# A hybrid decoder layer with 32 routed experts: the load order of the experts is made ahead of the gates, and the affine step of the first LayerNorm moves to GpSimd

## The chip, the cores and the metric

The kernel runs on one core of one Trainium2 chip. The metric is the device time of one execution, in microseconds (us); lower is better. The engines are called by their names here: TensorE (PE in the rows, PEld its weight loads), VectorE (DVE), ScalarE (ACT), GpSimd (POOL) and SyncE (SP), whose queue issues most of the DMA transfers.

## The reference, cut to what matters

One decoder layer on 512 tokens of 1024 channels, all in float32: four token mixers, a LayerNorm, a mixture of experts, a second LayerNorm. Only the end of it bears on this change:

```python
x = layer_norm(alpha * x + m @ w_out, ln1_g, ln1_b)
y = hierarchical_moe(x, ...)              # 32 experts of 1024x512, 1024x512, 512x1024
out = layer_norm(alpha * x + y, ln2_g, ln2_b)

# hierarchical_moe: top-1 of 4 groups, then top-2 of its 8 experts, per token
expert = g_sel * 8 + e_sel                # (512, 2)
gate = pg_top * pe_top / pe_top.sum(-1)
# for each expert e, over the tokens routed to it:
h = silu(xe @ w_gate[e]) * (xe @ w_up[e])
y[token] += gate * (h @ w_down[e])
```

No token is dropped: a loop behind the main part takes what does not fit the places below.

## The kernel before

The mixers and the output product take the first 740 us or so. Then come the experts, in 13 tiles of up to 128 rows (`moe`, L1157). The first two tiles hold the four experts 0 to 3, two experts each with 64 rows, so their weights can be loaded before the routing is known. The other 28 experts are laid on 11 tiles (`TILES`) with strips of 32 to 96 rows; which expert gets which place is decided by its rank when the experts are sorted by how many tokens they have. `K.plan` holds, by place, the rank that the place takes, and its first row and capacity.

For each tile, `expert_block` (L1056) makes the gate product `pg` and the up product `pu` on TensorE, `hh` = Silu(`pg`) * `pu` (Silu on ScalarE, the product on VectorE, L1078), transposes `hh`, makes the down product `py`, and adds it to `acc`, row by row, through a product with the gates (`combine`, L1113; `yh` and `yl` are the two halves of `py` in the format that this product takes). Two callbacks fill the gaps: `early` right behind `hh`, and `late` behind the transposes. In the first tile, `early` makes the gates (`gates`, L878), then the matrices of slots and gates (`slot_gates`, L1000, VectorE only: two comparisons with a slot number, scaled by the gate, and a sum, for each of four token blocks) and the affine step of the first norm, `acc` = ALPHA * (`acc` * g1 + b1) (`affine`, L1847); `late` makes the rest of the routing (`router`, L901). `tc.issue_after(x)` puts what it encloses behind x in the order; the engines' orders come from a scheduler that runs when the kernel is built. Each engine works through its own order and waits where an input or a buffer isn't ready.

The weights come in pieces of 1 MB, six for each expert, on SyncE's queue (`load`, L1725). They turn through 16 buffers, w0 to w15, of which the first ten hold pieces that are loaded during the mixers: piece n goes to buffer n mod 16 as soon as the last product with that buffer's piece is done. Pieces 0 to 11 are those of the first tile (gate 0 to 3, up 4 to 7, down 8 to 11), 12 to 23 of the second, and piece 24 is the first of the routed experts. So piece 24 needs w8, which the down product of the first tile frees halfway, and piece 36 needs w4, which the down product of the second tile frees halfway. From piece 24 on, SyncE reads the number of the expert from `R.order` (`rord`):

```python
es = [num(R.order[0:1, o + i:o + i + 1]) for i in range(ne)]      # L1241
```

In `router`, `rord` comes last of a chain on VectorE, with one product of it on GpSimd (L954): a key for each expert, all pairs of keys compared (28 x 28 on each partition, `rsq`), their sums, which are the ranks, then the base and capacity of each expert, and then the experts by place. The chain stands behind `hh` of the first tile.

Of the kernel before, what the change touches and what calls it, by code (L numbers as in the profile page):

```python
# [7 lines left out]
F32 = mybir.dt.float32  # L8
F32R = mybir.dt.float32r
BF16 = mybir.dt.bfloat16  # L10
I32 = mybir.dt.int32
U32 = mybir.dt.uint32
AF = mybir.ActivationFunctionType
OP = mybir.AluOpType
AX = mybir.AxisListType
PSUM = bass.MemoryType.PSUM

P = 128
# [3 lines left out]
NB = T // P  # L22
ALPHA = 2.0 ** 0.25
# [729 lines left out]
NE = 32  # L753
DE = 512
CAP = 64
NS = 4
ND = NE - NS
# [120 lines left out]
def gates(K, R):  # L878

    V, A = K.nc.vector, K.nc.scalar  # L880
    sb = K.rwk
    s4 = lambda n: sb.tile([P, 4], F32, name=n)
    bc = lambda t, n: t.unsqueeze(2).to_broadcast([P, 4, n])
    gl = R.lg[:, :, 0:4]
    gm, m1, m2 = (R.m[:, i] for i in range(3))
    ge = sb.tile([P, 4, 4], F32, name="rge")
    V.tensor_tensor(ge, gl, bc(gm, 4), op=OP.subtract)
    A.activation(ge, ge, AF.Exp)
    gs = s4("rgs")
    V.tensor_reduce(gs, ge, axis=AX.X, op=OP.add)  # L890
    e2 = s4("re2")
    V.tensor_tensor(e2, m2, m1, op=OP.subtract)
    A.activation(e2, e2, AF.Exp)
    den = s4("rden")
    V.scalar_tensor_tensor(den, e2, 1.0, gs, op0=OP.add, op1=OP.mult)
    R.g = [K.rsb.tile([P, 4], F32, name=f"rgt{j}") for j in range(2)]
    V.reciprocal(R.g[0], den)
    V.tensor_tensor(R.g[1], R.g[0], e2, op=OP.mult)


def router(K, R):  # L901

    nc = K.nc
    V, G, A = nc.vector, nc.gpsimd, nc.scalar
# [2 lines left out]
    OH = [R.oh[:, j] for j in range(2)]  # L907
    pos = R.pos
    cnt = pos[:, 4, :]

    ds_ = slice(NS, NE)
    row = lambda n, w=NE: sb.tile([P, w], F32, name=n)
    key = row("rkey", ND)
    V.scalar_tensor_tensor(key, cnt[:, ds_], float(NE), K.iof[:, ds_], op0=OP.mult, op1=OP.subtract)
    sq = sb.tile([P, ND, ND], F32, name="rsq", tag="rsq", bufs=1)
    V.tensor_tensor(sq, key[:, None, :].to_broadcast([P, ND, ND]), key.unsqueeze(2).to_broadcast([P, ND, ND]),
                    op=OP.is_gt)
    rank = row("rrank", ND)
    V.tensor_reduce(rank, sq, axis=AX.X, op=OP.add)

    at = lambda: V.tensor_tensor(sq, rank[:, None, :].to_broadcast([P, ND, ND]),
                                 K.plan[:, 0].unsqueeze(2).to_broadcast([P, ND, ND]), op=OP.is_equal)
    at()
    V.tensor_tensor(sq, sq, K.plan[:, 1].unsqueeze(2).to_broadcast([P, ND, ND]), op=OP.mult)
    V.tensor_reduce(key, sq.rearrange("p q e -> p e q"), axis=AX.X, op=OP.add)

# [14 lines left out]
    for j in range(2):  # L941
# [7 lines left out]
        V.tensor_tensor(sl, sl, ov, op=OP.add)  # L949
        R.slot.append(sl)  # L950
        lf.append((l_, ov))

    at()
    G.tensor_tensor(sq, sq, K.iof[:, None, ds_].to_broadcast([P, ND, ND]), op=OP.mult)  # L954
    V.tensor_reduce(key, sq, axis=AX.X, op=OP.add)
    R.order = keep.tile([P, ND], I32, name="rord")
    V.tensor_copy(R.order, key)

    nbk, over = row("rnbk"), row("rover")
    V.tensor_tensor(over, cnt, cap, op=OP.subtract)  # L960
# [196 lines left out]
def moe(K, xh, xl, out_acc, R, d0, affine, rest, load, load_rows, load_cols, small, last, ews):  # L1157
# [3 lines left out]
    nc, tc = K.nc, K.tc  # L1161
# [73 lines left out]
    for pr, tl in enumerate(tiles):  # L1235
# [35 lines left out]
        def early(after):  # L1271
            if pr == 0:
                with tc.issue_after(d0[1].end.ins):
                    gates(K, R)
            gts.extend(slot_gates(K, sj, R.g, h * P))
            if end:
                with tc.issue_after(K.send):
                    root()
            if pr == 0:
                with tc.issue_after(K.gend):  # L1280
                    affine()

        def late(after):
            nonlocal xe
# [184 lines left out]
def layer_kernel(tc, a, out):  # L1469
# [12 lines left out]
    with top:  # L1482
# [362 lines left out]
        K.osb = K.rsb  # L1845

        def affine():  # L1847
            for b in range(NB):
                V.scalar_tensor_tensor(acc[:, b, :], acc[:, b, :], ALPHA, g1, op0=OP.mult, op1=OP.mult)
            with tc.issue_after(K.xend):  # L1850
                A.mul(b1, b1, ALPHA)
            for b in range(NB):
                G.tensor_tensor(acc[:, b, :], acc[:, b, :], b1, op=OP.add)
            rst.close()

# [67 lines left out]
```

## Time and profile before

| | us |
|---|---|
| median of 3 runs | 1234.81 (1234.26 to 1236.95) |
| the profiled execution | 1239.61 |
| its span | 1237.8 |
| busy in the span: TensorE | 1150.0 (93%) |
| VectorE | 644.8 (52%) |
| ScalarE | 352.8 (29%) |
| GpSimd | 139.4 (11%) |

All rows are of the profiled execution, with times from the start of its span. A timeline row gives the start, the length, the engine, the line and the operation with its output and inputs; x4 behind it means four instructions merged, and then the length goes from the first start to the last end. A length includes what an instruction waits after it has begun. Starts and lengths are the profiler's; where one ends after the next has begun, the two overlap in the engine's pipeline.

### The profile page before, as it was taken

The numbers are of one execution on the slowest core, as the hardware profiler recorded it, in microseconds if no ns is written. First come the engines' busy times: TensorE is split into PE (matmuls) and PEld (weight loads), VectorE is DVE, ScalarE is ACT, GpSimd is POOL, SyncE is SP. The second block draws the span as 40 slices with busy tenths as digits, with TensorE's granted clock in tenths as the row PEclk, the third lists the DMA queues.
The fourth block names the chain that finished last, engine by engine and source line by source line (L and its number), as shares of the span: only waits on it lengthen the run. The fifth ranks groups of instructions, "written<-read, shape, count | busy, mean of one in ns | idle before, by whom it ended". The sixth has DMA issues, their size and how long they took to land.

```text
span 1237.8 us, 18955 instructions
## 1 busy us (share of the span) xinstructions
PE 1150.0 (93%) x6991; PEld 777.0 (63%) x6991; DVE 644.8 (52%) x1769; ACT 352.8 (29%) x752; POOL 139.4 (11%) x192
## 2 busy tenths in 40 slices
PE   7999999999999999999999988998999789987993
PEld 6768788888876776888888983532544234532542
DVE  6488878522239884334435489751444224432247
ACT  5433434333334444333334452100111011110012
POOL 4021322100000000212211044000000000000003
PEclk9999999999999999999999998999999999999996
DMA  7311212456652111656553238899999999999991
GB/s 185 89 41 33 44 29 70 132 181 192 188 177 64 52 36 40 216 162 192 179 172 122 94 116 326 348 421 420 421 422 420 421 420 421 421 421 421 420 340 70
DMA packets 108699, 276.65 MB, mean 224 GB/s; under 512 B 19393, under 2 KB 74780, under 8 KB 86076
## 3 DMA queue, kind: packets, MB, share of 16 engines
q1 hardware_dynamic: 90604, 252.79, 54.8%
q10 hardware_dynamic: 16768, 19.82, 5.0%
q0 software_dynamic: 1232, 2.81, 0.7%
q8 instruction: 56, 0.92, 0.3%
q14 instruction: 39, 0.32, 0.1%
HBM read 263.71 MB, written 11.67 MB: 222 GB/s over the span
## 4 chain that ended last, share of the span: by engine, by line
PE 68%; DMA 17%; DVE 9%; issue 2%; ACT 1%; POOL 1%; SPq 1%; ACTq 0%; DVEq 0%; POOLq 0%
PE mm L1382 9%; PE mm L1380 9%; PE mm L1381 9%; DMA w<-in_e_gate 6%; PE pu L1071 5%; DMA w<-in_e_down 5%; PE py L1101 4%; PE pg L1071 4%; DMA w<-in_e_up 3%; PE pm L1034 2%; PE pm L1036 2%; PE pm L1116 1%; PE pm L1117 1%; PE po L1705 1%; PE po L1706 1%
## 5 line engine op out<-in xcount | busy, mean ns | idle before, releaser
L1154 DVE TENSOR_TENSOR wlo<-wraw,whi 128x512 fp32r<-128x512 f32 (+2 forms) x180 | 123.1, 686 | 194.8 <-ACT whi L1151 193.3
L1380 PE MATMUL mm<-xh,whi 128*128 128x512 f32 x496 | 200.1, 404 | 2.5 <-ACT pc L1535 1.4
L1382 PE MATMUL mm<-xh,wlo 128*128 128x512 f32 x496 | 201.3, 406 | 0.0
L1381 PE MATMUL mm<-xl,whi 128*128 128x512 f32 x496 | 199.1, 401 | 0.0
L1151 ACT CAST whi<-wraw 128x512 fp32r<-128x512 f32 (+2 forms) x180 | 109.9, 612 | 205.9 <-PE mm L1381 142.1
L1124 DVE TENSOR_TENSOR acc<-acc,pm 128x512 f32<-128x512 f32 (+1 forms) x106 | 64.3, 655 | 111.3 <-PE pm L1117 111.3
L1101 PE MATMUL py<-w,hT 128*32 128x512 f32 (+2 forms) x608 | 114.8, 578 | 7.5 <-DMA w<-in_e_down 7.2
L1071 PE MATMUL pu<-w,xe 128*32 128x512 f32 (+1 forms) x576 | 104.6, 596 | 12.9 <-DMA w<-in_e_up 12.9
L1071 PE MATMUL pg<-w,xe 128*32 128x512 f32 (+1 forms) x576 | 101.4, 598 | 10.0 <-DMA w<-in_e_gate 10.0
L1380 PEld LDWEIGHTS mm<-xh,whi 128*128 128x128 f32 x496 | 94.1, 190 | 25.9 <-ACT pc L1535 2.7
L1382 PEld LDWEIGHTS mm<-xh,wlo 128*128 128x128 f32 x496 | 94.0, 190 | 22.3 <-issue 1.6
L1381 PEld LDWEIGHTS mm<-xl,whi 128*128 128x128 f32 x496 | 94.2, 190 | 21.7 <-issue 1.7
L1101 PEld LDWEIGHTS py<-w,hT 128*32 128x32 f32 (+1 forms) x608 | 35.2, 123 | 78.1 <-issue 56.4
L1071 PEld LDWEIGHTS pu<-w,xe 128*32 128x32 f32 (+1 forms) x576 | 29.2, 121 | 80.5 <-issue 54.9
L1071 PEld LDWEIGHTS pg<-w,xe 128*32 128x32 f32 (+1 forms) x576 | 30.6, 122 | 76.0 <-issue 55.0
L1034 PE MATMUL pm<-D,xh 128*128 128x256 f32 (+1 forms) x224 | 53.9, 283 | 1.2 <-DVE D L995 1.2
L1036 PE MATMUL pm<-D,xl 128*128 128x256 f32 (+1 forms) x224 | 53.8, 283 | 0.0
L1122 POOL TENSOR_TENSOR acc<-acc,yo 128x256 f32<-128x256 f32 x6 | 4.3, 732 | 438.2 <-ACT yo L1121 438.2
L1078 DVE TENSOR_TENSOR hh<-hh,pu 128x512 f32<-128x512 f32 x13 | 8.9, 686 | 79.6 <-PE pu L1071 79.6
L1109 ACT ACTIVATE yh<-py,dg 128x512 fp32r<-128x512 f32 x24 | 16.5, 686 | 116.3 <-PE py L1101 99.6
L1711 POOL TENSOR_TENSOR mT<-mT,th 128x512 f32<-128x512 f32 x24 | 35.7, 1486 | 123.6 <-DVE th L1710 122.6
L1401 PE MATMUL mm<-wlo,xh 128*128 128x256 f32 (+1 forms) x160 | 46.7, 292 | 0.0
(640 smaller groups left out, 2040.3 us busy)
## 6 DMA issues: line engine op xcount, KB each, us to landing
w<-in_e_gate SPq DMA_DIRECT2D x60, 1024.0 KB, 19.8
w<-in_e_down SPq DMA_DIRECT2D x58, 1024.0 KB, 19.8
w<-in_e_up SPq DMA_DIRECT2D x58, 1024.0 KB, 19.8
wraw<-in_w_in SPq DMA_DIRECT2D x128, 256.0 KB, 2.9
w<-in_e_up SPq DMA_DIRECT2D x12, 512.0 KB, 15.9
w<-in_e_down SPq DMA_DIRECT2D x12, 512.0 KB, 8.4
wraw<-in_w_branch SPq DMA_DIRECT2D x16, 256.0 KB, 2.6
w<-in_e_gate SPq DMA_DIRECT2D x8, 512.0 KB, 5.3
```

Source lines behind the costliest of these rows:

```text
L1034: TE.matmul(ps[:, i, :], self.xh[:, kt, b * P:b * P + P], D[:, b, :], start=i == 0 and b == 0, stop=False, skip_group_check=True)
L1036: TE.matmul(ps[:, i, :], self.xl[:, kt, b * P:b * P + P], D[:, b, :], start=False, stop=i == per - 1 and b == NB - 1, skip_group_check=True)
L1071: end = TE.matmul(ps[c, :], xe[:, kt, c], w(e, kind, kt, 0, T), start=kt == 0, stop=kt == 7, skip_group_check=True)
L1101: TE.matmul(at(c0, c1)[c, :], hT[:, f, c], w(e, 2, f, c0, c1), start=f == 0 and c0 % T == 0, stop=f == 3 and c1 % T == 0, skip_group_check ...
L1124: V.tensor_tensor(o, o, ps, op=OP.add)
L1151: nc.scalar.copy(hi, src)
L1154: nc.vector.tensor_tensor(lo, src, hi.bitcast(F32), op=OP.subtract)
L1380: TE.matmul(ps[i], hi[:, k, cs], self.xh[:, kk, :], start=kk == 0, stop=False)
L1381: TE.matmul(ps[i], hi[:, k, cs], self.xl[:, kk, :], start=False, stop=False)
L1382: end = TE.matmul(ps[i], lo[:, k, cs], self.xh[:, kk, :], start=False, stop=kk == 7)
L1401: TE.matmul(ps[:, :n], self.xh[:, kk, s], lo[:, k, :], start=False, stop=False)
L1711: G.tensor_tensor(mT[:, j, :], mT[:, j, :], th, op=OP.add)
```

## The change

Three things are moved. The ranks and the load order become a function of their own, `load_order`, which runs ahead of `gates` on VectorE, right behind the last `xe` (the gathered inputs of the experts); it works on the 28 x 28 pairs in two halves, and its one product on GpSimd becomes VectorE's. `router` keeps only the bases and capacities, from the ranks that are there. The affine step leaves VectorE: ScalarE scales both g1 and b1 by ALPHA, right behind its last `xe`, and GpSimd multiplies `acc` by one and adds the other. It no longer stands behind the slot gates.

```diff
--- before.py
+++ after.py
@@ -898,6 +898,35 @@
     V.tensor_tensor(R.g[1], R.g[0], e2, op=OP.mult)
 
 
+def at_place(K, R, sq, places=slice(0, ND)):
+
+    K.nc.vector.tensor_tensor(sq, R.rank[:, None, :].to_broadcast(sq.shape),
+                              K.plan[:, 0, places].unsqueeze(2).to_broadcast(sq.shape), op=OP.is_equal)
+
+
+def load_order(K, R):
+
+    V = K.nc.vector
+    sb, keep = K.rwk, K.rsb
+    ds_ = slice(NS, NE)
+    key = sb.tile([P, ND], F32, name="rkey")
+
+    V.scalar_tensor_tensor(key, R.pos[:, 4, ds_], float(NE), K.iof[:, ds_], op0=OP.mult, op1=OP.subtract)
+    nh = ND // 2
+    sq = sb.tile([P, nh, ND], F32, name="rsqh")
+    R.rank = keep.tile([P, ND], F32, name="rrank")
+    for h in (slice(0, nh), slice(nh, ND)):
+        V.tensor_tensor(sq, key[:, None, :].to_broadcast([P, nh, ND]), key[:, h].unsqueeze(2).to_broadcast([P, nh, ND]),
+                        op=OP.is_gt)
+        V.tensor_reduce(R.rank[:, h], sq, axis=AX.X, op=OP.add)
+    for h in (slice(0, nh), slice(nh, ND)):
+        at_place(K, R, sq, h)
+        V.tensor_tensor(sq, sq, K.iof[:, None, ds_].to_broadcast([P, nh, ND]), op=OP.mult)
+        V.tensor_reduce(key[:, h], sq, axis=AX.X, op=OP.add)
+    R.order = keep.tile([P, ND], I32, name="rord")
+    K.oend = V.tensor_copy(R.order, key).ins
+
+
 def router(K, R):
 
     nc = K.nc
@@ -907,20 +936,11 @@
     OH = [R.oh[:, j] for j in range(2)]
     pos = R.pos
     cnt = pos[:, 4, :]
-
     ds_ = slice(NS, NE)
     row = lambda n, w=NE: sb.tile([P, w], F32, name=n)
     key = row("rkey", ND)
-    V.scalar_tensor_tensor(key, cnt[:, ds_], float(NE), K.iof[:, ds_], op0=OP.mult, op1=OP.subtract)
     sq = sb.tile([P, ND, ND], F32, name="rsq", tag="rsq", bufs=1)
-    V.tensor_tensor(sq, key[:, None, :].to_broadcast([P, ND, ND]), key.unsqueeze(2).to_broadcast([P, ND, ND]),
-                    op=OP.is_gt)
-    rank = row("rrank", ND)
-    V.tensor_reduce(rank, sq, axis=AX.X, op=OP.add)
-
-    at = lambda: V.tensor_tensor(sq, rank[:, None, :].to_broadcast([P, ND, ND]),
-                                 K.plan[:, 0].unsqueeze(2).to_broadcast([P, ND, ND]), op=OP.is_equal)
-    at()
+    at_place(K, R, sq)
     V.tensor_tensor(sq, sq, K.plan[:, 1].unsqueeze(2).to_broadcast([P, ND, ND]), op=OP.mult)
     V.tensor_reduce(key, sq.rearrange("p q e -> p e q"), axis=AX.X, op=OP.add)
 
@@ -949,12 +969,6 @@
         V.tensor_tensor(sl, sl, ov, op=OP.add)
         R.slot.append(sl)
         lf.append((l_, ov))
-
-    at()
-    G.tensor_tensor(sq, sq, K.iof[:, None, ds_].to_broadcast([P, ND, ND]), op=OP.mult)
-    V.tensor_reduce(key, sq, axis=AX.X, op=OP.add)
-    R.order = keep.tile([P, ND], I32, name="rord")
-    V.tensor_copy(R.order, key)
 
     nbk, over = row("rnbk"), row("rover")
     V.tensor_tensor(over, cnt, cap, op=OP.subtract)
@@ -1271,14 +1285,15 @@
         def early(after):
             if pr == 0:
                 with tc.issue_after(d0[1].end.ins):
+                    load_order(K, R)
+                with tc.issue_after(K.oend):
                     gates(K, R)
             gts.extend(slot_gates(K, sj, R.g, h * P))
             if end:
                 with tc.issue_after(K.send):
                     root()
             if pr == 0:
-                with tc.issue_after(K.gend):
-                    affine()
+                affine()
 
         def late(after):
             nonlocal xe
@@ -1845,11 +1860,11 @@
         K.osb = K.rsb
 
         def affine():
-            for b in range(NB):
-                V.scalar_tensor_tensor(acc[:, b, :], acc[:, b, :], ALPHA, g1, op0=OP.mult, op1=OP.mult)
             with tc.issue_after(K.xend):
+                A.mul(g1, g1, ALPHA)
                 A.mul(b1, b1, ALPHA)
             for b in range(NB):
+                G.tensor_tensor(acc[:, b, :], acc[:, b, :], g1, op=OP.mult)
                 G.tensor_tensor(acc[:, b, :], acc[:, b, :], b1, op=OP.add)
             rst.close()
 
```

VectorE's order behind the gathered inputs `xe`, before. `rge`, `re`, `rgs`, `rden` and `rgt` are the steps of the gates, `g` and `G` those of the slot gates.

```order
L1047 TENSOR_SCALAR xe<-pm,ln1c 128x256 x4
L887 TENSOR_TENSOR rge<-lg,rm_6901 128x16
L892 TENSOR_TENSOR re_7851<-rm_6901 128x4
L890 TENSOR_REDUCE rgs<-rge 128x4
L895 SCALAR_TENSOR_TENSOR rden<-re_7851,rgs 128x4
L897 RECIPROCAL rgt_7856<-rden 128x4
L898 TENSOR_TENSOR rgt_7857<-rgt_7856,re_7851 128x4
L1009 TENSOR_SCALAR g_7860<-iof,rsl_6900,rgt_7856 128x128
```

The same place now, up to the load order:

```order
L914 SCALAR_TENSOR_TENSOR rkey<-rpos,iof 128x28
L919 TENSOR_TENSOR rsqh<-rkey 128x392
L921 TENSOR_REDUCE rrank<-rsqh 128x14
L919 TENSOR_TENSOR rsqh<-rkey 128x392
L921 TENSOR_REDUCE rrank<-rsqh 128x14
L903 TENSOR_TENSOR rsqh<-rrank,plan 128x392
L924 TENSOR_TENSOR rsqh<-rsqh,iof 128x392
L925 TENSOR_REDUCE rkey<-rsqh 128x14
L903 TENSOR_TENSOR rsqh<-rrank,plan 128x392
L924 TENSOR_TENSOR rsqh<-rsqh,iof 128x392
L925 TENSOR_REDUCE rkey<-rsqh 128x14
L927 CAST rord<-rkey 128x28
```

Eleven instructions and the cast to `rord` stand between `xe` and the first step of the gates (`rge`, which follows next).

VectorE's order around `hh` of the first tile, before:

```order
L1011 TENSOR_TENSOR G<-G,g_7870 128x128
L1009 TENSOR_SCALAR g_7875<-iof,rsl_6900,rgt_7856 128x128
L1011 TENSOR_TENSOR G<-G,g_7875 128x128
L1849 SCALAR_TENSOR_TENSOR acc<-acc,g_7788 128x1024 x4
L1009 TENSOR_SCALAR g_8087<-iof,rsl_6900,rgt_7856 128x128
L1078 TENSOR_TENSOR hh<-hh,pu 128x512
L914 SCALAR_TENSOR_TENSOR rkey<-rpos,iof 128x28
L928 TENSOR_SCALAR rbase<-iof 128x4
L929 MEMSET rcap 128x4
L916 TENSOR_TENSOR rsq<-rkey 128x784
```

And now:

```order
L1025 TENSOR_TENSOR G<-G,g_7886 128x128
L1023 TENSOR_SCALAR g_7891<-iof,rsl_6900,rgt_7872 128x128
L1025 TENSOR_TENSOR G<-G,g_7891 128x128
L1023 TENSOR_SCALAR g_8095<-iof,rsl_6900,rgt_7872 128x128
L1092 TENSOR_TENSOR hh<-hh,pu 128x512
L903 TENSOR_TENSOR rsq<-rrank,plan 128x784
L948 TENSOR_SCALAR rbase<-iof 128x4
L949 MEMSET rcap 128x4
L944 TENSOR_TENSOR rsq<-rsq,plan 128x784
```

The four affine steps ahead of `hh` are gone, and so are the key `rkey` and the first comparisons behind it.

GpSimd's order at the affine step, before (`xl` belongs to the norm, the product with `iof` to the load order, the last row to the last tile):

```order
L1440 DMA g_7788<-in_ln_g 128x1024
L1440 DMA b_7789<-in_ln_b 128x1024
L1801 TENSOR_TENSOR xl<-acc,xh 128x8x64 x2
L1853 TENSOR_TENSOR acc<-acc,b_7789 128x1024 x4
L954 TENSOR_TENSOR rsq<-rsq,iof 128x784
L1122 TENSOR_TENSOR acc<-acc,yo 128x256 x6
```

And now:

```order
L1455 DMA g_7788<-in_ln_g 128x1024
L1455 DMA b_7789<-in_ln_b 128x1024
L1816 TENSOR_TENSOR xl<-acc,xh 128x8x64 x2
L1867 TENSOR_TENSOR acc<-acc,g_7788 128x1024 x2
L1868 TENSOR_TENSOR acc<-acc,b_7789 128x1024 x2
L1867 TENSOR_TENSOR acc<-acc,g_7788 128x1024 x2
L1868 TENSOR_TENSOR acc<-acc,b_7789 128x1024 x2
L1136 TENSOR_TENSOR acc<-acc,yo 128x256 x6
```

Eight affine instructions stand there instead of four, with nothing of VectorE's ahead of them. SyncE's order stays as it was. On TensorE one group moves: the products of the first tile's first `combine` stand behind three products of the second tile's `pu`, and not behind eleven.

## Rows read from the trace of the kernel before

**Rows 1.** The page of the kernel before: what the DMA engines moved in each of the 40 slices of the span (31 us each), and the pieces of gate weights that SyncE issues at L1729.

```profile
GB/s 185 89 41 33 44 29 70 132 181 192 188 177 64 52 36 40 216 162 192 179 172 122 94 116 326 348 421 420 421 422 420 421 420 421 421 421 421 420 340 70
...
w<-in_e_gate SPq DMA_DIRECT2D x60, 1024.0 KB, 19.8
```

**Rows 2.** Three stretches of the span: length, then busy time and instructions of each engine, the granted share of TensorE's full clock, the mean share of the 16 DMA engines, and what they moved.

```profile
768.50:777.50 9.00, 9.00 (x46) 2.93 (x44) 9.00 (x26) 0.00 (x0) 1.85 (x1) 1.00 0.02 7
777.50:805.00 27.50, 26.36 (x150) 15.74 (x148) 19.71 (x65) 4.71 (x8) 0.00 (x0) 1.00 0.99 399
805.00:1195.00 390.00, 351.79 (x2074) 153.67 (x2068) 142.10 (x326) 39.84 (x65) 0.00 (x0) 1.00 1.01 419
```

**Rows 3.** Who waited for whom on SyncE's DMA queue, over the whole span: total us, times, longest us.

```profile
SPq L1164 <- DVE rlf L945: 18.0, 1, 18.0
...
SPq L1729 <- PE py L1101: 17.4, 11, 12.0
```

**Rows 4.** SyncE's timeline: start and length in us, the issues merged. The last row is from a narrower window.

```profile
753.93 4.24 SPq L1729 DMA_DIRECT2D w<-in_e_down  x4
776.66 6.58 SPq L1729 DMA_DIRECT2D w<-in_e_gate  x8
...
805.03 0.91 SPq L1729 DMA_DIRECT2D w<-in_e_up  x2
```

**Rows 5.** VectorE's timeline from the end of the gathered inputs on: start, length, line, operation, and in brackets idle time of the engine just before.

```profile
742.08 1.96 DVE L1047 TENSOR_SCALAR xe<-pm,ln1c 128x256 f32<-128x256 f32 x4 [0.90 <-PE pm L1036]
743.95 0.17 DVE L887 TENSOR_TENSOR rge<-lg,rm 128x16 f32<-128x16 f32 x1
746.20 0.17 DVE L890 TENSOR_REDUCE rgs<-rge 128x4 f32<-128x16 f32 x1 [2.01 <-ACT rge L888]
746.97 0.34 DVE L1009 TENSOR_SCALAR g<-iof,rsl,rgt 128x128 f32<-128x128 f32 x1
...
750.33 8.95 DVE L1849 SCALAR_TENSOR_TENSOR acc<-acc,g 128x1024 f32<-128x1024 f32 x4
759.20 2.36 DVE L1009 TENSOR_SCALAR g<-iof,rsl,rgt 128x128 f32<-128x128 f32 x1
761.48 0.67 DVE L1078 TENSOR_TENSOR hh<-hh,pu 128x512 f32<-128x512 f32 x1
762.08 1.75 DVE L914 SCALAR_TENSOR_TENSOR rkey<-rpos,iof 128x28 f32<-128x28 f32 x1
...
766.85 0.96 DVE L921 TENSOR_TENSOR rsq<-rrank,plan 128x784 f32<-128x784 f32 x1
...
772.00 1.92 DVE L1010 TENSOR_SCALAR G<-iof,rsl,rgt 128x128 f32<-128x128 f32 x1
...
775.70 0.16 DVE L957 CAST rord<-rkey 128x28 int32<-128x28 f32 x1
...
776.08 0.40 DVE L962 TENSOR_TENSOR ro<-rover,thr 128x256 f32<-128x256 f32 x1
```

**Rows 6.** TensorE's timeline: up product of the first tile, transposes of `hh`, down products of the first and of the second tile.

```profile
750.30 7.04 PE L1071 MATMUL pu<-w,xe 128*64 128x512 f32 x32
...
762.21 1.13 PE L1083 MATMUL pm<-ident,hh 128*128 128x128 f32 x4 [4.02 <-DVE hh L1078]
...
765.89 8.33 PE L1101 MATMUL py<-w,hT 128*64 128x512 f32 x32
...
801.36 7.09 PE L1101 MATMUL py<-w,hT 128*64 128x512 f32 x32
```

**Rows 7.** ScalarE's timeline.

```profile
742.65 1.99 ACT L1045 ACTIVATE xe<-pm,ln1c 128x256 f32<-128x256 f32 x4 [5.33 <-DVE xe L1047]
...
746.17 1.04 ACT L1851 ACTIVATE b<-b 128x1024 f32<-128x1024 f32 x1
...
780.81 0.68 ACT L1109 ACTIVATE yh<-py,dg 128x512 fp32r<-128x512 f32 x1
```

**Rows 8.** GpSimd's timeline; the two rows of L1853 are from narrower windows, each of two instructions of the four.

```profile
727.92 3.11 POOL L1801 TENSOR_TENSOR xl<-acc,xh 128x512 fp32r<-128x512 f32 x2 [5.92 <-ACT xh L1800]
...
736.32 3.16 POOL L1801 TENSOR_TENSOR xl<-acc,xh 128x512 fp32r<-128x512 f32 x2 [0.91 <-DVE roh L858]
...
754.86 6.62 POOL L1853 TENSOR_TENSOR acc<-acc,b 128x1024 f32<-128x1024 f32 x2
...
758.15 5.64 POOL L1853 TENSOR_TENSOR acc<-acc,b 128x1024 f32<-128x1024 f32 x2
...
771.99 1.85 POOL L954 TENSOR_TENSOR rsq<-rsq,iof 128x784 f32<-128x784 f32 x1 [8.20 <-DVE rsq L921]
```

**Rows 9.** VectorE's timeline: single instructions beside GpSimd's. The last row is from a narrower window.

```profile
730.16 0.19 DVE L845 TENSOR_REDUCE rm<-rel 128x1 f32<-128x32 f32 x1
...
736.52 1.42 DVE L857 TENSOR_TENSOR rohs<-rel,rel 128x32 bf16<-128x32 f32 x1
737.87 1.66 DVE L859 TENSOR_TENSOR roh<-rel,rel 128x32 f32<-128x32 f32 x1
...
755.91 3.37 DVE L1849 SCALAR_TENSOR_TENSOR acc<-acc,g 128x1024 f32<-128x1024 f32 x1
```

**Rows 10.** Two stretches of one microsecond, columns as in rows 2.

```profile
762.00:763.00 1.00, 0.79 (x4) 0.79 (x5) 1.00 (x2) 0.00 (x0) 1.00 (x1) 0.50 0.96 401
...
768.00:769.00 1.00, 1.00 (x6) 0.26 (x4) 1.00 (x3) 0.00 (x0) 0.00 (x0) 0.76 0.46 188
```

## The prediction

> **What bounds the kernel now.** Read first the page's slices: TensorE looks like the bound, but the rate of the DMA engines tells more [rows 1]. From slice 26 to slice 37 (counting from 0) it stands at 420 to 422 GB/s; the two slices ahead of that have only 326 and 348. The table of stretches makes both exact [rows 2]: from 805 to 1195 us the sixteen DMA engines are full (share 1.01, 419 GB/s), and from 768.5 to 777.5 us they move next to nothing (7 GB/s). The full stretch is the stream of expert weights, in pieces of 1024 KB (1.049 MB), so 2.5 us each at 419 GB/s. A stream that never pauses again hands every delay at its head to the end of the kernel, and every gain too. So the question is when the stream starts, and whether it stays full.
>
> Next, SyncE's queue, which issues the stream. Its longest wait there is 18.0 us for `rord`, the load order (the view names a VectorE neighbour, L945), and then 12.0 us for the down product `py` of the second tile [rows 3]. In order of time [rows 4]: the last four pieces of fixed experts go out from 753.93 to 758.17, the first routed piece (piece 24, counting from 0) at 776.66, and piece 36 at 805.03. In between, 399 GB/s over 27.5 us [rows 2] is what a full stream moves in 26.2 us, so the routed stream counts as full from 778.8, 2.1 us behind its first issue. Twelve pieces (24 to 35) last to 808.8; piece 36 was issued 3.8 us ahead of that, 1.7 us earlier than it had to be. The head of the stream thus has two conditions: piece 24 needs the order and slot w8, which the first tile's `py` frees; piece 36 needs w4, which the second tile's `py` frees.
>
> Third, VectorE, on whose queue both hang [rows 5]. `xe` is done about 744; gates and slot gates follow (the last from 746.97 to 750.33); four affine instructions 750.33 to 759.28; one more slot gate 2.36; then `hh` at 761.48, on which TensorE waits: its up product ended at 757.34, and the transposes of `hh` start at 762.21, `py` at 765.89 [rows 6]. `rord` is written at 775.70, last of a chain begun at 762.08.
>
> **The change, part by part.** *The order goes ahead of the gates.* The twelve instructions cost 5.8 us by themselves: a 784-element comparison takes 0.96 and a 256-element one 0.40 [rows 5], so 0.55 for the 392 of a half (estimated between the two); ten of these make 5.5, the key and the cast 0.16 to 0.17 each like their narrow neighbours. With nothing in the way `rord` would stand at 749.8, and even with the waits below at about 757.5, when SyncE is still issuing fixed pieces (to 758.17). So the wait of 18.0 us is gone. The next thing that is late is w8. In the router behind `hh`, the key, one square, two reductions, one comparison and the cast fall away; nothing on TensorE waits there soon enough to count, so I book nothing.
>
> *The affine moves to GpSimd.* VectorE loses 8.95 us ahead of `hh`. GpSimd gets eight instructions of 128x1024 instead of four, and no longer waits for VectorE: ScalarE scales g1 right behind its last `xe` (744.64), one such product takes 1.04 [rows 7], so GpSimd starts at 745.75, while VectorE is in the middle of the order. That start decides, because the two engines do not run side by side here. GpSimd's third affine ends at 761.48 and its fourth at 763.79 [rows 8]; VectorE's fourth affine lasts from 755.91 to 759.28, 3.37 long, and ends 1.1 behind 758.15, where GpSimd's second ends and its third begins [rows 8, 9]. The slot gate at 759.20 takes 2.36 instead of 0.34 and ends with GpSimd's third; the key at 762.08 takes 1.75 for 28 elements and ends with its fourth. A 0.34 us gate at 772.00 takes 1.92 beside a GpSimd product of 1.85 [rows 5, 8]. And they take turns: of two adjacent comparisons of 32 elements, the one at 736.52 ends with the first of two GpSimd instructions and the one at 737.87 with the second [rows 8, 9]. Not all are held: the reduction at 730.16 takes 0.19 inside a GpSimd instruction, and `hh`, one of whose inputs lies in PSUM, takes 0.67 at 761.48 [rows 5, 8, 9].
>
> GpSimd's own time for 128x1024 follows from the turns: 761.48 less 759.28 is 2.20, 763.79 less 761.56 is 2.23. I take 2.2, so eight are 17.6 us.
>
> Now the sum for `hh`. VectorE's own work from 743.95 to `hh` is 10.6: order 5.8, six gate instructions 1.0, slot gates 3.4 (746.97 to 750.33), one more 0.3, rounding. Of that, 1.8 runs before GpSimd starts; 2.2 (three half reductions, the cast, a narrow reduction, the reciprocal) runs beside it; 2.7 (four half comparisons and products at 0.55, three narrow ones at 0.17) gets one turn each between GpSimd's eight; 3.9 follows. So `hh` starts at 745.75 + 17.6 + 2.7 + 3.9 = 770.0 instead of 761.48: **8.5 us later**, though VectorE has less to do. ScalarE's two exponentials, the table loads around them and the Silu fit into the waits.
>
> TensorE's steps behind `hh` move with it. Its clock fell in the idle time before the transposes to 0.50, its 1.2 GHz level, and came back to 2.4 GHz within 768 to 769, after six microseconds of work [rows 10]; I take the same after the longer pause. Full-speed `py` is 7.09 [rows 6], so half of the first one was done at 765.89 + 8.33 - 3.5 = 770.7, now 779.2; 2.1 behind that the stream is full at 781.3 (before: 778.8), and twelve pieces last to 811.3. Piece 36: 805.03 + 8.5 = 813.5, and 0.7 more, as the first combine now stands after three products of the second tile's up product and not eleven, while `yh` still follows that tile's Silu (780.81 before) [rows 7]; with 2.1 that is 816.3, against 808.8. The stream pauses a second time, and what follows is **7.5 us late**. Behind that the slots are freed in time: piece 40 needed only the next gate product, nine microseconds later too, with four pieces of 2.5 us ahead of it.
>
> The profiled execution took 1239.61 us, 4.8 more than the median of the runs, 1234.81; the difference is added to the median: 1234.8 + 7.5 = **1242.3**.
>
> Ends of this sum: without the 0.7, and 1.5 for the 2.1, it is +6.2. If GpSimd's products cost what 1.85 for 784 elements [rows 8] scales to, 2.4, four of eight give 0.8 more; if the clock stays low through all of the first `py`, some 2 us more. So +5 to +10: 1240 to 1245.
>
> The page "SBUF — State Buffer" of the Trainium skill, section "SBUF: two separate sides", states that VectorE and GpSimd share one pair of ports under an exclusive lock held for a whole instruction, by VectorE for two SBUF inputs or a two-port mode. The rows agree in what is held (the slot gate's 2.36) and what not (`hh`, 0.67). It does not say who is next: taken without turns, it leads to the third rival.
>
> **The rivals.** *One, faster: VectorE goes first.* If its instructions passed GpSimd's whenever they were ready, or GpSimd's started late, the order, gates and slot gates would end by 754.6 (756.6 with the 2.0 wait for the exponential [rows 5]) and `hh` would wait only for the up product: 757.4, 4.1 earlier than now. TensorE would hardly idle, its clock would stay up, and about 3.0 come back (1.2 in `py`, half of the 3.7 between the transposes and `py`). Piece 36 is then ready at 805.0 - 4.1 - 3.0 + 0.7 + 2.1 = 800.7; the fixed pieces' stream ends at 768.5 and twelve more at 798.5. Gain 8.1: 1226.7. For it: the hole of 9 us is real and the order is early enough. Against it: every turn in [rows 8, 9]. It decides at the break-even point, `hh` 1.0 later than now, 762.5. Chance 0.15.
>
> *Two, no change: several VectorE instructions per turn.* With four, about half of GpSimd's work is passed before `hh`, which comes near 762; piece 36 starts about where it does now: 1235. For it: the turns seen are few; against it, the two adjacent comparisons did not pass together. Chance 0.08.
>
> *Three, slower still: no turns.* GpSimd's eight hold VectorE from its first held instruction, 746.4, to 763.35, and 8.2 to 8.6 of its work follow: `hh` at 772, 10.5 late, the stream 9.5: 1244.3. The two adjacent comparisons speak against it [rows 9]. Chance 0.12.
>
> **How the numbers follow.** The forecast has 0.65. A measurement tells about 0.2% (2.5 us) from no change; forecast and third rival are slower by more, 0.77; faster 0.15; same 0.08. The range 1232 to 1246 holds the forecast with its ends and rivals two and three, and leaves out the faster case.
>
> **What would show it.** In the profile after: SyncE waits for the first `py`, not for `rord`; GpSimd's affine starts near 745.8 and ends near 766; VectorE's half comparisons and gates last 2 us and more, one per GpSimd instruction; `hh` near 770, piece 24 near 779, piece 36 near 814, with a short pause of the DMA engines ahead of it; then 419 GB/s to the end. I am wrong if `hh` comes before 763, or if the second pause is missing.

## The result, and the profile after

The changed kernel is slower: median 1245.16 us (four runs, 1242.50 to 1246.02) against 1234.85, a ratio of 1.0073 with a 95% interval of 1.0055 to 1.0091. Twelve later runs of the same kernel, again beside the kernel before, gave 1.0045 (1.0025 to 1.0065). So the loss is between 3 and 11 us; the forecast was 7.5. One of the twelve runs of the kernel called e4_vector_only below took 2557.12 us, where the others lie between 1229.45 and 1239.03, and stands in no ratio; why it took so long isn't shown.

The profiled execution took 1244.92 us, its span 1243.2. It ended its `xe` 0.5 us earlier than the profile of before (743.54 against 744.04, from VectorE's rows), so times of the two traces are compared from there. First the stretches of the DMA engines, which answer to [rows 2] (same columns):

```profile
768.50:778.00 9.50, 8.46 (x34) 3.75 (x36) 9.33 (x33) 0.58 (x1) 0.00 (x0) 0.73 0.01 3
778.00:808.80 30.80, 29.50 (x164) 16.61 (x162) 17.24 (x55) 4.70 (x8) 0.00 (x0) 1.00 1.00 408
808.80:812.70 3.90, 3.90 (x22) 1.33 (x20) 3.90 (x15) 0.00 (x0) 0.00 (x0) 1.00 0.19 36
812.70:1195.00 382.30, 344.88 (x2044) 151.49 (x2040) 137.77 (x317) 37.13 (x61) 0.00 (x0) 1.00 1.01 418
```

The pause at the head is still there, and a second one has opened from 808.8 to 812.7, where before the stream was full. Next SyncE's timeline (the last row from a narrower window), which answers to [rows 4], and then who waited for whom on its queue from 740 to 815 us (total, times, longest), which answers to [rows 3]:

```profile
753.43 4.24 SPq L1744 DMA_DIRECT2D w<-in_e_down  x4
777.03 9.77 SPq L1744 DMA_DIRECT2D w<-in_e_gate  x8
...
811.49 0.91 SPq L1744 DMA_DIRECT2D w<-in_e_up  x2
```

```profile
SPq L1744 <- PE py L1115: 36.3, 4, 18.1
...
SPq L1178 <- DVE rge L887: 0.7, 1, 0.7
```

Nothing of any length waits for the order any more (0.7 us, named by a VectorE neighbour). The wait of 18.0 us is gone, and one of 18.1 us for the first tile's `py` stands in its place. Counted from the end of `xe`, piece 24 goes 33.5 us later (before 32.6), and piece 36, the row at 811.49, 68.0 us (before 61.0). Now the timelines of VectorE, which answers to [rows 5], and of GpSimd, which answers to [rows 8]:

```profile
746.06 2.01 DVE L903 TENSOR_TENSOR rsqh<-rrank,plan 128x392 f32<-128x392 f32 x1
748.11 2.60 DVE L924 TENSOR_TENSOR rsqh<-rsqh,iof 128x392 f32<-128x392 f32 x1
750.75 0.56 DVE L925 TENSOR_REDUCE rkey<-rsqh 128x14 f32<-128x392 f32 x1
751.34 2.02 DVE L903 TENSOR_TENSOR rsqh<-rrank,plan 128x392 f32<-128x392 f32 x1
753.39 2.60 DVE L924 TENSOR_TENSOR rsqh<-rsqh,iof 128x392 f32<-128x392 f32 x1
...
756.63 1.61 DVE L927 CAST rord<-rkey 128x28 int32<-128x28 f32 x1
758.16 0.16 DVE L887 TENSOR_TENSOR rge<-lg,rm 128x16 f32<-128x16 f32 x1
758.24 2.30 DVE L892 TENSOR_TENSOR re<-rm 128x4 f32<-128x4 f32 x1
...
760.82 2.03 DVE L895 SCALAR_TENSOR_TENSOR rden<-re,rgs 128x4 f32<-128x4 f32 x1 [0.19 <-ACT re L893]
...
763.09 2.06 DVE L898 TENSOR_TENSOR rgt<-rgt,re 128x4 f32<-128x4 f32 x1
...
768.80 0.68 DVE L1092 TENSOR_TENSOR hh<-hh,pu 128x512 f32<-128x512 f32 x1
```

```profile
745.21 5.07 POOL L1867 TENSOR_TENSOR acc<-acc,g 128x1024 f32<-128x1024 f32 x2 [6.25 <-issue]
...
760.49 4.64 POOL L1868 TENSOR_TENSOR acc<-acc,b 128x1024 f32<-128x1024 f32 x2
```

On VectorE read the lengths, which no longer go by the size: a half comparison takes 2.01, a half reduction 0.56, and the 4-element subtraction at 758.24 takes 2.30. Eight are long (all rows but the reduction, `rge` and `hh`), as many as GpSimd has, and GpSimd's eight last from 745.21 to 765.13, without a gap. None of the eight reads or writes a tile that GpSimd's do, so what holds them is no input. One more passed: `rge`, with two inputs in the SBUF, took 0.16 right behind the held cast. After 765.13 nothing is held, and `hh` comes 3.7 us later. TensorE's timeline, which answers to [rows 6], and two stretches that answer to [rows 10]:

```profile
762.75 1.97 PE L1085 MATMUL pg<-w,xe 128*64 128x512 f32 x2 [5.91 <-ACT hh L1091]
769.54 1.12 PE L1097 MATMUL pm<-ident,hh 128*128 128x128 f32 x4 [4.83 <-DVE hh L1092]
...
773.21 7.22 PE L1115 MATMUL py<-w,hT 128*64 128x512 f32 x32
...
807.81 7.09 PE L1115 MATMUL py<-w,hT 128*64 128x512 f32 x32
```

```profile
760.00:773.00 13.00, 5.42 (x14) 2.40 (x16) 12.43 (x26) 2.67 (x4) 5.12 (x3) 0.50 0.63 263
773.00:774.00 1.00, 1.00 (x6) 0.38 (x4) 1.00 (x2) 0.00 (x0) 0.00 (x0) 0.71 0.00 0
```

TensorE stood idle for 5.91 us ahead of the first row and for 4.83 more ahead of the transposes of `hh`. Its granted clock was 0.50, its 1.2 GHz level, from 760 to 773, and came back with the first products of `py`, which took 7.22. The second `py` starts at 807.81, 64.3 us after `xe` (before 57.3).

### The profile page after: what moved, and what is told of

Its sections match the earlier page's. It is cut to its first block, busy times and chain, and to the rows that moved or that the text cites. A ratio compares the mean times of both kernels' runs of the same rounds, so it can differ in the third digit from the quotient of the medians.

```text
span 1243.2 us, 18962 instructions
## 1 busy us (share of the span) xinstructions
PE 1149.6 (92%) x6991; PEld 776.8 (62%) x6991; DVE 648.3 (52%) x1771; ACT 353.4 (28%) x753; POOL 144.6 (12%) x195
## 4 chain that ended last, share of the span: by engine, by line
PE 67%; DMA 20%; DVE 8%; issue 2%; POOL 1%; ACT 1%; SPq 0%; ACTq 0%; DVEq 0%; POOLq 0%
PE mm L1397 9%; PE mm L1395 9%; PE mm L1396 9%; DMA w<-in_e_gate 6%; DMA w<-in_e_down 6%; DMA w<-in_e_up 5%; PE py L1115 4%; PE pu L1085 4%; PE pg L1085 4%; PE pm L1048 2%; PE pm L1050 2%; PE mm L1416 1%; PE po L1720 1%; PE po L1721 1%; PE po L1719 1%
## 5 line engine op out<-in xcount | busy, mean ns | idle before, releaser
L1138 DVE TENSOR_TENSOR acc<-acc,pm 128x512 f32<-128x512 f32 (+1 forms) x106 | 64.3, 656 | 112.2 <-PE pm L1131 112.2
L1115 PE MATMUL py<-w,hT 128*32 128x512 f32 (+2 forms) x608 | 111.4, 574 | 5.6 <-DMA w<-in_e_down 5.3
L1396 PEld LDWEIGHTS mm<-xl,whi 128*128 128x128 f32 x496 | 94.4, 190 | 21.6 <-issue 1.5
## 6 DMA issues: line engine op xcount, KB each, us to landing
w<-in_e_gate SPq DMA_DIRECT2D x60, 1024.0 KB, 19.8
w<-in_e_down SPq DMA_DIRECT2D x58, 1024.0 KB, 19.8
w<-in_e_up SPq DMA_DIRECT2D x58, 1024.0 KB, 19.9
```

Of the source, the lines that this page charges most:

```text
L1115: TE.matmul(at(c0, c1)[c, :], hT[:, f, c], w(e, 2, f, c0, c1), start=f == 0 and c0 % T == 0, stop=f == 3 and c1 % T == 0, skip_group_check ...
L1138: V.tensor_tensor(o, o, ps, op=OP.add)
L1396: TE.matmul(ps[i], hi[:, k, cs], self.xl[:, kk, :], start=False, stop=False)
```

## The experiments

All counts below start at the end of the first `xe`, since the stretch ahead of it varies from run to run. "Without loads" is what is missing from a full DMA share in the 100 one-microsecond stretches from there, and "last load" is the first issue behind the last expert's weights. In the three runs e4 and e8, two of the 32 products of the second `py` go some 10 us ahead of the rest; the column has the start of the other 30. Ratios are against runs of the kernel before on the same chip; 0.001 is 1.24 us.

| run | `hh` | piece 24 | second `py` | last load | us without loads | ratio, 95% interval |
|---|---|---|---|---|---|---|
| before | 17.4 | 32.6 | 57.3 | 452.0 | 11.0 | |
| e0_before_again | 17.4 | 32.6 | 58.9 | 451.5 | 10.5 | 0.9992, 0.9976 to 1.0009 |
| after | 25.3 | 33.5 | 64.3 | 457.8 | 15.0 | 1.0073, 1.0055 to 1.0091 |
| after_again | 25.3 | 34.0 | 64.7 | 458.3 | 15.6 | 1.0045, 1.0025 to 1.0065 |
| e1_order_only | 19.7 | 27.6 | 60.4 | 453.9 | 11.4 | 1.0016, 1.0001 to 1.0032 |
| e2_affine_only | 23.2 | 37.8 | 62.5 | 456.7 | 15.4 | 1.0043, 1.0028 to 1.0058 |
| e3_no_affine | 13.5 | 19.9 | 50.6 | 443.9 | 2.3 | 0.9949, 0.9930 to 0.9968 |
| e6_four_on_gpsimd | 18.1 | 26.0 | 55.9 | 449.1 | 6.2 | 0.9982, 0.9962 to 1.0002 |
| e7_memset | 13.7 | 20.1 | 50.9 | 444.3 | 2.6 | (one run) |
| e4_vector_only | 13.4 | 19.8 | 55.0 | 447.6 | 5.5 | 0.9979, 0.9958 to 1.0000 |
| e4_again | 13.4 | 19.8 | 54.8 | 447.6 | 5.7 | 0.9977, 0.9959 to 0.9995 |
| e8_two_ahead | 13.4 | 19.8 | 51.5 | 443.9 | 2.0 | 0.9931, 0.9910 to 0.9951 |

The theory: VectorE and GpSimd take turns, one held instruction of VectorE's for each of GpSimd's, and `hh` and all behind it pay for that. The main rival: the order step itself costs, by the VectorE work that it puts ahead of `hh`.

### The two kernels once more

> The kernel before, unchanged, for a second profile. Its first profiled execution took 1239.6 us where the runs of it have their median at 1234.85, so the profiles of before and after lie 5.3 us apart and the medians 10.3. If that first profile was the odd one, this one takes about 1235 us, with `hh` still near 761.5, piece 24 near 776.7 and piece 36 near 805.0 counted from its own start, and the missing 5 us show in one other stretch. If a profile of this kernel always costs it some 5 us, it comes out near 1239.6 again. The ratio to itself should be 1.000, within 0.002.

> The kernel after, unchanged, in more runs and for a second profile. Its four runs gave +10.3 us by the medians (ratio 1.0073, from 1.0055 to 1.0091), while its trace, counted from the end of `xe` to the last load, is only 5.9 us longer than that of the kernel before (457.8 against 452.0), with 15.0 us without loads against 11.0. If the trace holds all of the loss, the ratio comes out near 1.005, the low edge of the first interval. If some 3 to 4 us of the loss lie elsewhere, it stays near 1.007, and a second profile shows a longer stretch ahead of `xe` or behind the last load than those of the kernels before.

The second profiled execution of before took 1240.5 us, but the median of that kernel's runs is 1236.0: neither was a median run. Their stages agree where it counts (`hh` at 17.4, 11.0 and 10.5 us without loads). Not all repeats: in the second, TensorE waited 1.66 us for `yl` (0.35 in the first), the second `py` came 1.6 us later, and piece 36 went 62.6 us after `xe` (61.0), which cost nothing visible, as the first profile left piece 36 1.7 us to spare. Most of what differs between runs lies ahead of `xe`: its end stood between 738.7 and 746.3 us in the twelve profiles of this study, in code that is the same up to there. The second profile of after repeats the first to 0.6 us in every column. So the trace shows a loss of 5.8 to 6.8 us (457.8 and 458.3 against 452.0 and 451.5), and the runs' 9.0 and 5.6 (ratio less 1, times 1236) lie on both sides of it. The new ratio is the 1.005 that was expected if the trace holds all of the loss. Why the first four runs gave 3 us more isn't shown; the two intervals overlap.

### The order alone

```diff
 # the affine step as in the kernel before; the order ahead of the gates as after
+for b in range(NB):
+    V.scalar_tensor_tensor(acc[:, b, :], acc[:, b, :], ALPHA, g1, ...)
 with tc.issue_after(K.xend):
-    A.mul(g1, g1, ALPHA)
     A.mul(b1, b1, ALPHA)
 for b in range(NB):
-    G.tensor_tensor(acc[:, b, :], acc[:, b, :], g1, op=OP.mult)
     G.tensor_tensor(acc[:, b, :], acc[:, b, :], b1, op=OP.add)
...
-    affine()
+    with tc.issue_after(K.gend):
+        affine()
```

> The order step ahead of the gates as in the kernel after; the affine step as before (four VectorE instructions behind the slot gates, four additions on GpSimd). Theory (the time is lost because GpSimd's eight products and sums hold VectorE): without them the half order step costs VectorE about 10.6 us ahead of `hh`, of which some 9 come back since the affine work no longer stands ahead of it; `hh` near 763, piece 24 near 777.5, time 0 to +2 us against before. Rival (the order step itself is what costs, since it puts some 10 us of VectorE ahead of the gates and of all that TensorE waits for): `hh` near 769 as in the kernel after, time +6 us or more.

Measured +2.0 us (0.1 to 4.0), `hh` at 19.7 where the theory had 19 and the rival 25. The rival falls as the main cause; a small cost is left. Piece 24 came 5 us earlier than before, which the expectation had wrong (it had it later), and nothing was gained by it. The timelines of VectorE and TensorE in this run, and one stretch with the columns of [rows 2]:

```profile
759.02 2.54 DVE L903 TENSOR_TENSOR rsq<-rrank,plan 128x784 f32<-128x784 f32 x1
761.48 2.31 DVE L948 TENSOR_SCALAR rbase<-iof 128x4 f32<-128x4 f32 x1
...
779.43 1.34 PE L1131 MATMUL pm<-yl,DT 128*128 128x512 f32 x3 [2.72 <-DVE yl L1124]
```

```profile
798.50:804.00 5.50, 5.50 (x31) 2.19 (x31) 5.15 (x17) 0.56 (x1) 0.00 (x0) 1.00 0.13 21
```

GpSimd's last two sums hold two router instructions (2.54, 2.31), TensorE waits 2.72 us for `yl`, the second `py` starts 60.4 us after `xe` (before 57.3 and 58.9), and the stream stands still ahead of it (21 GB/s). Here the early first issue bought a second pause.

### The affine step alone

```diff
 # the router and its order as in the kernel before
-for b in range(NB):
-    V.scalar_tensor_tensor(acc[:, b, :], acc[:, b, :], ALPHA, g1, ...)
 with tc.issue_after(K.xend):
+    A.mul(g1, g1, ALPHA)
     A.mul(b1, b1, ALPHA)
 for b in range(NB):
+    G.tensor_tensor(acc[:, b, :], acc[:, b, :], g1, op=OP.mult)
     G.tensor_tensor(acc[:, b, :], acc[:, b, :], b1, op=OP.add)
...
-    with tc.issue_after(K.gend):
-        affine()
+    affine()
```

> The affine step on GpSimd as in the kernel after; the order step in its old place, behind the gates in the router. Theory (GpSimd's eight instructions and VectorE's take turns): the gates' and slot gates' VectorE instructions between 747 and 765 are held as long as GpSimd has one of its own under way, `hh` near 767, the order leaves at about 780, piece 24 near 781, time +4 to +5 us against before, more than half of the whole loss. Rival (the order step costs): `hh` no later than 761.5, since four VectorE products of 2.0 us are gone, time 0 to -3 us.

Measured +5.3 us (3.5 to 7.2), `hh` at 23.2 (expected 767 less 744.04, 23.0). VectorE's timeline, then GpSimd's:

```profile
749.52 2.65 DVE L1010 TENSOR_SCALAR G<-iof,rsl,rgt 128x128 f32<-128x128 f32 x2
...
766.14 2.33 DVE L1011 TENSOR_TENSOR G<-G,g 128x128 f32<-128x128 f32 x1
768.51 0.35 DVE L1009 TENSOR_SCALAR g<-iof,rsl,rgt 128x128 f32<-128x128 f32 x1
```

```profile
749.62 4.78 POOL L1851 TENSOR_TENSOR acc<-acc,g 128x1024 f32<-128x1024 f32 x2 [8.72 <-issue]
```

Other instructions than in the kernel after are held here, those of the slot gates, 128 elements wide, and again eight: the second of the first row (2.3 of its 2.65 us) and seven more up to the one at 766.14, each at 2.2 to 2.5. When GpSimd is done, the same kind takes 0.35 (768.51). So it is the move to GpSimd that costs, whatever VectorE has to do there, and although it takes 8.95 us of work from VectorE.

### Without the affine step

```diff
 with tc.issue_after(K.xend):
-    A.mul(g1, g1, ALPHA)
-    A.mul(b1, b1, ALPHA)
-for b in range(NB):
-    G.tensor_tensor(acc[:, b, :], acc[:, b, :], g1, op=OP.mult)
-    G.tensor_tensor(acc[:, b, :], acc[:, b, :], b1, op=OP.add)
```

> The kernel after without the affine step of the first norm: it is left out of the result, to price it. Theory (turns): every VectorE instruction of the order step has the length that it has alone (the two halves of `at_place` and the products by the expert numbers some 0.56 us in place of 2.0 and 2.6, the cast well under 0.2 in place of 1.6), `hh` near 757, piece 24 no later than in the kernel before, time -6 to -9 us against before. Rival (the order step itself costs): the long instructions stay long, `hh` near 768, time +6 us or more.

This kernel leaves the affine step out of the result, so it shows a price and is no version to use. VectorE's timeline:

```profile
748.82 0.57 DVE L903 TENSOR_TENSOR rsqh<-rrank,plan 128x392 f32<-128x392 f32 x1
749.42 0.57 DVE L924 TENSOR_TENSOR rsqh<-rsqh,iof 128x392 f32<-128x392 f32 x1
...
752.42 0.18 DVE L927 CAST rord<-rkey 128x28 int32<-128x28 f32 x1
...
759.74 0.69 DVE L1092 TENSOR_TENSOR hh<-hh,pu 128x512 f32<-128x512 f32 x1 [2.19 <-PE pu L1085]
```

Measured -6.3 us (-8.7 to -4.0). The same instructions that took 2.01, 2.60 and 1.61 in the kernel after take 0.57, 0.57 and 0.18; `hh` waits 2.19 us for TensorE instead of the other way round; the stream hardly pauses (2.3 us). `hh` at 13.5 is close to the 13.0 expected (757 less 744.04), and the gain is at the low end of the 6 to 9 us. The order by itself, from its key to its cast, lasts 6.4 us (746.21 to 752.60).

### Half of GpSimd's instructions

```diff
 for b in range(NB):
     G.tensor_tensor(acc[:, b, :], acc[:, b, :], g1, op=OP.mult)
-    G.tensor_tensor(acc[:, b, :], acc[:, b, :], b1, op=OP.add)
+with tc.issue_after(K.hend):
+    for b in range(NB):
+        V.tensor_tensor(acc[:, b, :], acc[:, b, :], b1, op=OP.add)
```

> Half the dose: as the kernel after, but GpSimd does only the four products by `g`; VectorE adds `b` itself in four instructions behind `hh`. Theory (strict turns, one held VectorE instruction for each GpSimd instruction): exactly four VectorE instructions are long (the two of `at_place` and the two products by the expert numbers, 2.0 to 2.6 us); the cast, the additions and products of the gates are short again, 0.16 to 0.18; `hh` comes about 17.9 us after `xe` (25.3 less 1.4, 2.1, 1.9 and 1.9), time 0 to +4 us against before. Rival (what is long is long by its own kind, not by its turn): the cast and the gates' instructions stay at 1.6 to 2.3 us and `hh` stays at 25.

VectorE's timeline:

```profile
744.55 2.01 DVE L903 TENSOR_TENSOR rsqh<-rrank,plan 128x392 f32<-128x392 f32 x1
746.60 2.60 DVE L924 TENSOR_TENSOR rsqh<-rsqh,iof 128x392 f32<-128x392 f32 x1
...
749.82 2.00 DVE L903 TENSOR_TENSOR rsqh<-rrank,plan 128x392 f32<-128x392 f32 x1
751.86 2.60 DVE L924 TENSOR_TENSOR rsqh<-rsqh,iof 128x392 f32<-128x392 f32 x1
...
755.09 0.18 DVE L927 CAST rord<-rkey 128x28 int32<-128x28 f32 x1
...
755.27 0.16 DVE L892 TENSOR_TENSOR re<-rm 128x4 f32<-128x4 f32 x1
```

Exactly four are long; the cast is back at 0.18, the gates' subtraction at 0.16, `hh` at 18.1 where 17.9 was expected. So the number of held instructions follows GpSimd's, eight for eight and four for four. The time was expected at 0 to +4 and came out at -2.2 us (-4.7 to +0.2). What the trace shows for it: the four sums, 4.62 us behind `hh`, ran beside products that TensorE had to make anyway, no wait for `yl` opened, the first `py` took 7.03 us (before 8.33 and 7.30), and the second started at 55.9, earlier than before.

### Fills instead of products

```diff
 for b in range(NB):
-    G.tensor_tensor(acc[:, b, :], acc[:, b, :], g1, op=OP.mult)
-    G.tensor_tensor(acc[:, b, :], acc[:, b, :], b1, op=OP.add)
+    G.memset(g1, float(b))
+    G.memset(b1, float(b))
```

> The affine step is left out of the result; in its place GpSimd fills the two rows `g` and `b` with a constant, eight instructions of 128x1024 which read nothing from the SBUF (its 128x512 fills take 0.54 us in the trace, so about 1.05 each, 8.4 in all). If any GpSimd instruction in the SBUF takes turns with VectorE, up to eight VectorE instructions are held, each to about 1.0 us in place of 0.57 or less, and `hh` comes some 17 us after `xe`. If only its two-input instructions do, none is held, and `hh` comes 13.5 us after `xe`, as without the affine step.

This kernel too leaves the affine step out. VectorE's timeline, then GpSimd's:

```profile
744.36 0.57 DVE L924 TENSOR_TENSOR rsqh<-rsqh,iof 128x392 f32<-128x392 f32 x1
...
747.36 2.77 DVE L927 CAST rord<-rkey 128x28 int32<-128x28 f32 x1
747.45 2.68 DVE L887 TENSOR_TENSOR rge<-lg,rm 128x16 f32<-128x16 f32 x1
```

```profile
743.78 0.96 POOL L1868 MEMSET b<- 128x1024 f32 x1
...
747.36 0.94 POOL L1868 MEMSET b<- 128x1024 f32 x1
748.25 0.94 POOL L1867 MEMSET g<- 128x1024 f32 x1
749.15 0.94 POOL L1868 MEMSET b<- 128x1024 f32 x1
```

Neither expectation holds whole. The two-input product runs at 0.57 beside a fill, not held. But the cast, which has one input, is held for 2.77 us, through the last three fills, to 750.13; the two behind it in the queue (2.68 and 2.60) end with it. `hh` came at 13.7, so it cost next to nothing here.

### A version that beats both

```diff
 with tc.issue_after(K.xend):
-    A.mul(g1, g1, ALPHA)
     A.mul(b1, b1, ALPHA)
 for b in range(NB):
-    G.tensor_tensor(acc[:, b, :], acc[:, b, :], g1, op=OP.mult)
-    G.tensor_tensor(acc[:, b, :], acc[:, b, :], b1, op=OP.add)
+    V.scalar_tensor_tensor(acc[:, b, :], acc[:, b, :], ALPHA, g1, ...)
+    V.tensor_tensor(acc[:, b, :], acc[:, b, :], b1, op=OP.add)
...
-    affine()
+    with tc.issue_after(K.hend):
+        affine()
```

> The order step ahead of the gates, and the whole affine step on VectorE (four products of some 1.04 us and four sums of as much, 8.4 us) behind `hh` and ahead of the rest of the router; GpSimd does nothing there. Theory (GpSimd's turns cost, not the work): `hh` comes 13.5 us after `xe` as without the affine step, no VectorE instruction ahead of it is longer than its kind alone, piece 24 goes some 20 us after `xe`, and the 8.4 us fall on the rest of the router, where TensorE has products of its own to do; `yl` is late by some 3 us, the second tile's `py` comes 53 us after `xe` (before 57.3, without the step 50.6), time -3 to -7 us against before, faster than both kernels. Rival (what counts is the amount of VectorE work ahead of the second tile, wherever it stands): the second tile's `py` comes 59 us after `xe` (50.6 + 8.4), a pause of 4 to 6 us opens there, time 0 to +2.

> The run with the affine step wholly on VectorE behind `hh`, unchanged, beside the one with two products ahead of `hh`: its ratio was 0.9979, from 0.9958 to 1.0000, which leaves open whether it is faster than the kernel before. By its trace (5.5 us without loads against 11.0; 447.6 us from `xe` to the last load against 452.0 and 451.5) it should be 4 us faster, a ratio of 0.997; if the first interval's upper end is true, no faster at all.

The timelines of VectorE and TensorE in the first of these:

```profile
754.64 2.35 DVE L1867 SCALAR_TENSOR_TENSOR acc<-acc,g 128x1024 f32<-128x1024 f32 x2
...
780.67 1.19 PE L1131 MATMUL pm<-yl,DT 128*128 128x512 f32 x4 [2.83 <-DVE yl L1124]
```

Alone, VectorE needs 1.13 us for a product or a sum of 128x1024 (2.35 for two), where GpSimd's cost it a turn of 2 us and more each. All eight behind `hh` take 9.2 us. Measured -2.6 us (-5.2 to 0.0) and, again, -2.8 (-5.1 to -0.6): faster than both kernels, by little and at the low end of what was expected. TensorE waits 2.83 us for `yl` here, its granted clock is 0.50 for some 3 us behind that wait (782 to 785), and the second `py` comes at 55, not 53. The next step moves two of the products into the 2.2 us in which VectorE waits for `pu`:

```diff
 # against the run before this one; affine() itself now goes behind the slot gates
-for b in range(NB):
+for b in range(2):
     V.scalar_tensor_tensor(acc[:, b, :], acc[:, b, :], ALPHA, g1, ...)
-    V.tensor_tensor(acc[:, b, :], acc[:, b, :], b1, op=OP.add)
+with tc.issue_after(K.hend):
+    for b in range(2, NB):
+        V.scalar_tensor_tensor(acc[:, b, :], acc[:, b, :], ALPHA, g1, ...)
+    for b in range(NB):
+        V.tensor_tensor(acc[:, b, :], acc[:, b, :], b1, op=OP.add)
```

> As the run with the affine step wholly on VectorE, but two of its four products stand ahead of `hh`, in the 2.2 us in which VectorE waits there for TensorE's `pu`; the other two products and the four sums stay behind it. Theory (a piece of VectorE work costs only where VectorE is waited for): `hh` still comes about 13.5 us after `xe`, `yl` some 2.2 us earlier than the 39.3 of that run, TensorE's wait for it falls from 2.8 us to under 1, the second tile's `py` comes at 53 in place of 55, the time without loads falls from 5.5 us to about 3.5, time -3 to -6 us against before. Rival (`py` of the second tile is set by something else than `yl`): `py` stays at 55, the time without loads at 5.5, time as in that run, -1 to -4.

The timelines of VectorE and TensorE:

```profile
750.94 2.35 DVE L1867 SCALAR_TENSOR_TENSOR acc<-acc,g 128x1024 f32<-128x1024 f32 x2
...
753.59 0.69 DVE L1092 TENSOR_TENSOR hh<-hh,pu 128x512 f32<-128x512 f32 x1
754.20 2.35 DVE L1870 SCALAR_TENSOR_TENSOR acc<-acc,g 128x1024 f32<-128x1024 f32 x2
...
777.78 1.20 PE L1131 MATMUL pm<-yl,DT 128*128 128x512 f32 x4 [0.39 <-DVE yl L1124]
```

The two products end at 753.29, and `hh` starts at 753.59 without having been delayed (13.4 after `xe`, as without the affine step). TensorE's wait for `yl` is 0.39, its clock stays up, the second `py` comes at 51.5 and the stream is without loads for 2.0 us in all. Measured -8.5 us (-11.1 to -6.1), 1227.9 against 1236.9, more than the 3 to 6 expected: the products with `yl` come 2.5 us earlier, near the 2.2 expected, and TensorE gets from the first of them to the first two of the second `py` in 3.6 us (37.6 to 41.2 after `xe`), where the run before needed 4.7 (40.1 to 44.7), partly at the low clock. This version does all of the work, and its last load goes at 443.9, as without the affine step.

## Why the prediction was right, point by point

**The bound.** It holds: in the table the time goes with the us without loads, from 2.0 (-8.5 us) to 15.6 (+5.6), if not one to one (some 5 us fewer in the runs e4 were worth 2.6 to 2.8). The two conditions at the head of the stream hold too: the first `py` frees piece 24, the second one piece 36, and with twelve pieces between them the later condition counts.

**The order.** The wait of 18.0 us for it is gone and the next late thing is w8, as said. Its twelve instructions take 6.4 us and not 5.8: each half instruction costs 0.60 from start to start.

**The affine step.** GpSimd started 1.67 us after `xe` (said 1.71) and ended after 21.6 (said 22.0). Turns, one to one, were the step with the most weight on few rows, and the kernel after, the affine step alone, and the half dose show them with eight, eight and four. Wrong in detail: the cast was counted as running beside GpSimd, and it is held; `rge`, counted with a turn of its own, passed behind it in the same turn (0.16). So the number of turns came out as forecast by luck. And GpSimd's eight took 19.9 us from first start to last end, not 20.3: beside the half instructions its own 128x1024 takes 2.0 (10.33 us for four turns of the half dose, by GpSimd's row there, less four of 0.57), not 2.2. With 3.7 behind them instead of 3.9, `hh` came 25.3 us after `xe`, forecast 26.0.

**TensorE behind `hh`.** This term was mis-sized: the first `py` was taken at 8.33, as before, and took 7.22 and 7.67 in the two profiles, as the clock came back earlier in it. The 8.33 was one profile's: the second profile of the kernel before has 7.30. Piece 24 went at 33.5 instead of 35.2, 0.7 of that by `hh` and 1.0 by this term.

**The second pause.** It is there, 3.9 us long, and piece 36 went at 68.0 instead of 70.2 (forecast 814.2). So the trace lost 5.8 to 6.8 us where 7.5 was forecast: the mechanism held, with terms that were 1.7 us too large at piece 24. That the two measurements, 9.0 and 5.6, lie on both sides of 7.5 says little, as they differ by more from each other than the trace does from the forecast.

**The rivals.** VectorE going first is refuted by the eight long instructions. Its break-even, `hh` at 762.5, that is 18.5 after `xe`, fits the runs on either side: 18.1 gave -2.2 us, 19.7 gave +2.0. Several VectorE instructions per turn is refuted by the same eight: two in one turn stand there once, the cast and `rge`, and `hh` came at 25.3 and not near 18. The rival of no turns at all is refuted by the half instructions that pass between GpSimd's.

## What to carry to other kernels

Work moved to GpSimd is not free for VectorE: ask what VectorE runs meanwhile, and count one held instruction, as long as GpSimd's, for each product or sum that GpSimd issues while VectorE has instructions of the kinds named below, however short they are. Where the same work takes VectorE half as long, leave it there, and put it in the stretch where VectorE waits for something (2.2 us of waiting, filled, were worth some 6 here, part of it TensorE's clock). And before an early transfer is paid for, look for the next one that will wait: the order alone came 5 us sooner and gained nothing.

## What the runs showed of the hardware

Which VectorE instructions are held depends on what GpSimd does. Beside GpSimd's two-input products and sums, two-input instructions of VectorE were held (2.01 to 2.60), and so were ones with one wide input, a cast (1.61) and the slot gates' comparisons (2.2 to 2.4), but no reduction (0.56) and no `hh`, with one input in PSUM (0.67 beside a sum of GpSimd's in the kernel before [rows 5, 8], 0.68 in the run with the order alone). One two-input instruction, `rge`, passed in 0.16 behind the held cast. Beside fills, two-input instructions were free (0.57), unless they stood right behind the cast, which was held (2.77). The Trainium skill's page "SBUF — State Buffer", section "SBUF: two separate sides", states that an instruction of VectorE's with two SBUF inputs contends only with a GpSimd instruction that reads the SBUF; the 0.57 and 2.01 us agree.

Who is next differs too: between products and sums each held VectorE instruction waited for one of GpSimd's, while the cast waited through three fills on end. Why isn't shown, nor why `rge` passed.
